# Mixer stage: late low parts of the GLU operand, an input quarter in the preparation's tile, a later residual write

## The chip, the cores and the metric

One core of a Trainium2 chip runs the whole program; the metric is the device time of one execution in microseconds. The core's engines run side by side: TensorE (PE, its weight loads as PEld), VectorE (DVE), ScalarE (ACT), GpSimd (POOL) and SyncE (SP), which issues most DMAs. Each engine takes its own instructions in a fixed order; semaphores tie the engines together.

## The reference

One step of a two-layer encoder over 1024 prompt and 64 sample positions, width 1024. Layer 0 has an attention mixer, layer 1 a diagonal state-space (SSM) mixer, then a GELU and a gated unit (GLU); each layer ends in a gated convolutional FFN. The part that matters here:

```python
    def block(carry, u_blk):
        ...
        _, _, sr, si = lax.associative_scan(_affine_combine, (ar, ai, xr, xi), axis=1)
        y = jnp.einsum('blgp,gip->blgi', sr, cr) - jnp.einsum('blgp,gip->blgi', si, ci)
        return (sr[:, -1], si[:, -1]), y
    ...
    y = ys.transpose(1, 0, 2, 3, 4).reshape(b, t, D_MODEL) + d_skip.astype(jnp.float32) * h.astype(jnp.float32)
    z = jax.nn.gelu(y).astype(h.dtype)
    ag = z @ w_glu + b_glu
    out = ag[..., :D_MODEL] * jax.nn.sigmoid(ag[..., D_MODEL:])
```

## The kernel before, in words

The stages follow one another: attention, first FFN (with the SSM tables prepared beside it, `ssm_prep`), SSM mixer with GLU (`ssm`), second FFN. Positions are cut into three blocks of 384, 384 and 320 columns. A float32 product is three matmuls on split operands: each operand x is kept as a high half (a rounded copy, made by ACT) and a low half (x minus the high half, made by DVE), and of the four partial products low·low is left out.

**Scan stage.** `batch` (L1236) works on one or two of 32 group pairs q; there are 18 batches: q=0, q=1, fourteen pairs from q=2 to q=29, q=30, q=31. `staged` runs several batches at once, each some `yield`s behind the one before. A batch's tables `pm` are loaded by SP (L1222); PE makes `p` from `pm` and the inputs U (L1258); ACT makes `sc` and `rd` (L1266, L1270); DVE makes `wk` by L1289, L1294, L1295, the scan at L1306, and L1309, L1310; PE multiplies out into the `p3` tiles (L1318, L1324); ACT copies them to `ys` (L1332). The inputs come as four quarters U(0) to U(3) of 16 groups (`ssm_load`, L1187); U(2) takes the slot `ypB`, which holds block 2 of the first FFN's output y until that block is written to DRAM as the residual ("spill", L1561, called in the batch q=2 round).

**From ys to the GLU operand.** After every four q (one `kt` of 0 to 7) ACT issues the write `yd` of `ys` (L1339), SP reads it back in another layout as `yf` (L1344), ACT forms z (GELU, L1359 and L1362) and its high half `zh` (three blocks, L1368), DVE its low half `zl` (three blocks, L1372). The DVE subtractions for kt 0 to 5 stand between scan instructions. The high and low halves (`whl`, L217) of the first two GLU weight tiles are made in the last scan rounds too.

**GLU.** For m = 0 the six first kt are multiplied for the three blocks with all three products, pb's weight first, then kt 6, then kt 7; the later m follow. The order on each engine comes from the order of the code and the `order` calls; the Tile framework adds waits where a buffer slot is taken again: a new tile in a slot waits until all readers of the last one are done.

**Preparation.** Its tiles `w`, `tl` and `tp` (L1058, L1100) are three separate tiles in the pool `prep2`, which nothing uses after the preparation.

## Time and profile before

| | us |
|---|---|
| median of 3 runs | 2240.37 |
| lowest, highest | 2238.83, 2241.77 |
| profiled execution: time | 2241.03 |
| profiled execution: span, first to last instruction | 2239.2 |

The profiled execution is one run, 0.66 us above the median; its span is what the trace covers and the rest (1.8 us) lies around it. Over the span PE is busy 98%, DVE 74%, ACT 47%, POOL 18%. The scan stage runs from about 1190 to 1294, the GLU follows. Averages over the span say little of this stage: it has to be read by windows and by the order of the instructions.

### The profile page before, as it was taken

The page shows a single profiled execution, that of the slowest core. Times are in us where ns is not written, and L with a number is a line of the kernel's source. Part 1 is how long each engine was busy: PE and PEld are TensorE (multiplying, and loading weights), DVE is VectorE, ACT ScalarE, POOL GpSimd, SP SyncE. Part 2 cuts the span into 40 slices and gives each one's busy share as a digit, 9 for nine tenths or more (in the row PEclk, how much of TensorE's full clock was granted, in tenths as well). Part 3 has the DMA queues.
Part 4 walks back from the last instruction along what each step waited for, and adds up shares of the span by engine and source line. Part 5 has one row for each costly group of instructions (what it writes and reads, how often), then busy time and mean ns, then how long its engine had stood idle before and what let it go on. Part 6 is the DMA issues. An engine that isn't in the chain of part 4 may idle for free.

```text
span 2239.2 us, 35982 instructions
## 1 busy us (share of the span) xinstructions
PE 2191.6 (98%) x13875; PEld 2117.1 (95%) x13875; DVE 1661.3 (74%) x2886; ACT 1042.3 (47%) x1890; POOL 412.8 (18%) x474
## 2 busy tenths in 40 slices
PE   9999999999999999999988899999999999999997
PEld 8987789999999999999986699999999999999997
DVE  8687647989878877767758855597976776676764
ACT  5255747422343342555545641263555455455543
POOL 5322004200032423000200034352010110110000
PEclk9999999999999999999999899999999999999999
DMA  5100015655355565887749888752266686579772
GB/s 197 37 22 29 20 62 158 241 188 202 122 150 173 176 208 187 274 279 236 233 163 339 263 280 294 249 167 75 87 224 229 218 297 226 196 272 314 218 253 97
DMA packets 208123, 428.47 MB, mean 191 GB/s; under 512 B 23312, under 2 KB 114224, under 8 KB 205008
## 3 DMA queue, kind: packets, MB, share of 16 engines
q1 hardware_dynamic: 175648, 326.56, 44.2%
q0 software_dynamic: 23984, 95.12, 11.9%
q10 hardware_dynamic: 8320, 4.49, 0.8%
q8 instruction: 109, 1.79, 0.3%
q14 instruction: 62, 0.51, 0.1%
HBM read 297.75 MB, written 128.37 MB: 190 GB/s over the span
## 4 chain that ended last, share of the span: by engine, by line
PE 32%; DMA 13%; DVE 9%; issue 4%; ACT 2%; POOL 2%; SPq 0%; DVEq 0%; ACTq 0%; POOLq 0%
PE mm L224 10%; PE mm L226 10%; PE mm L225 10%; DMA sj<-in_w_up 3%; DMA raw<-in_w_down 2%; DMA jw<-in_w_down 2%; DMA raw<-sd 1%; POOL sj L1391 1%; DMA yd<-ys 1%; DVE whl L217 1%; DMA su<-sj 1%; DMA gd<-t 1%; DVE gt L564 1%; DVE t L425 1%; DMA yf<-yd 1%
## 5 line engine op out<-in xcount | busy, mean ns | idle before, releaser
L224 PE MATMUL mm<-hl,whl 128*128 128x384 f32 (+1 forms) x1960 | 643.3, 329 | 4.1 <-DVE hl L307 3.1
L226 PE MATMUL mm<-hh,whl 128*128 128x384 f32 (+1 forms) x1960 | 641.2, 329 | 2.3 <-DVE whl L217 2.3
L225 PE MATMUL mm<-hh,whl 128*128 128x384 f32 (+1 forms) x1960 | 643.1, 328 | 0.0
L224 PEld LDWEIGHTS mm<-hl,whl 128*128 128x128 f32 x1960 | 368.4, 188 | 6.5 <-DVE hl L307 4.7
L226 PEld LDWEIGHTS mm<-hh,whl 128*128 128x128 f32 x1960 | 368.4, 188 | 3.0 <-DVE whl L217 2.9
L225 PEld LDWEIGHTS mm<-hh,whl 128*128 128x128 f32 x1960 | 368.6, 188 | 0.1
L217 DVE TENSOR_TENSOR whl<-raw,whl 128x1024 fp32r<-128x1024 f32 x202 | 254.9, 1263 | 146.7 <-ACT whl L217 146.2
L217 ACT ACTIVATE whl<-raw 128x1024 fp32r<-128x1024 f32 x202 | 213.0, 1058 | 248.1 <-PE mm L226 128.6
L224 PE MATMUL mm<-gt,whl 128*128 128x384 f32 (+1 forms) x968 | 316.8, 327 | 2.9 <-ACT whl L217 2.4
L226 PE MATMUL mm<-gt,whl 128*128 128x384 f32 (+1 forms) x968 | 315.8, 327 | 0.7 <-DVE whl L217 0.7
L225 PE MATMUL mm<-gt,whl 128*128 128x384 f32 (+1 forms) x968 | 315.9, 327 | 0.0
L224 PEld LDWEIGHTS mm<-gt,whl 128*128 128x128 f32 x968 | 181.7, 188 | 3.7 <-ACT whl L217 2.6
L226 PEld LDWEIGHTS mm<-gt,whl 128*128 128x128 f32 x968 | 181.7, 188 | 1.2 <-DVE whl L217 1.2
L225 PEld LDWEIGHTS mm<-gt,whl 128*128 128x128 f32 x968 | 181.8, 188 | 0.0
L195 DVE TENSOR_TENSOR whl<-raw,whl 128x1024 fp32r<-128x1024 f32 x84 | 96.4, 1154 | 72.7 <-ACT whl L194 71.3
L424 DVE SCALAR_TENSOR_TENSOR t<-u,ppt,t 128x1090 f32<-128x1090 f32 x88 | 126.9, 1443 | 5.8 <-ACT t L423 4.1
L194 ACT ACTIVATE whl<-raw 128x1024 fp32r<-128x1024 f32 x84 | 82.6, 987 | 101.8 <-DMA raw<-sd 40.1
L423 ACT ACTIVATE t<-u,ppt 128x1090 f32<-128x1090 f32 x88 | 114.2, 1298 | 26.2 <-DVE u L520 13.6
L425 DVE SCALAR_TENSOR_TENSOR t<-u,ppt,t 128x1090 f32<-128x1090 f32 x88 | 122.0, 1386 | 0.4
L415 DVE TENSOR_TENSOR u<-rb,mm 128x384 f32<-128x384 f32 (+1 forms) x164 | 80.8, 504 | 31.2 <-PE mm L226 26.4
L438 ACT ACTIVATE t<-t 128x1090 f32<-128x1090 f32 x44 | 49.1, 1115 | 113.1 <-DVE t L425 113.1
L564 DVE TENSOR_TENSOR gt<-gr,gt 128x768 fp32r<-128x768 f32 (+2 forms) x106 | 90.5, 881 | 11.1 <-ACT gt L563 10.2
(389 smaller groups left out, 4141.5 us busy)
## 6 DMA issues: line engine op xcount, KB each, us to landing
raw<-in_w_up SPq DMA_DIRECT2D x88, 512.0 KB, 4.4
raw<-in_w_down SPq DMA_DIRECT2D x74, 512.0 KB, 4.4
raw<-sd SPq DMA_DIRECT2D x40, 512.0 KB, 4.9
sj<-in_w_up POOLq DMA_DIRECT2D x68, 256.0 KB, 6.1
su<-sj POOLq DMA_DIRECT2D x34, 512.0 KB, 5.9
raw<-su SPq DMA_DIRECT2D x34, 512.0 KB, 4.6
pm<-prm SPq DMA_DIRECT2D x32, 522.0 KB, 8.2
gr<-td SPq DMA_DIRECT2D x40, 384.0 KB, 5.6
```

Source lines behind the costliest of these rows:

```text
L194: nc.scalar.activation(w[:, 0], raw, AF.Copy)
L195: nc.vector.tensor_sub(w[:, 1], raw, w[:, 0].bitcast(F32))
L217: x = nc.scalar.activation(w[:, 0], raw, AF.Copy), nc.vector.tensor_sub(w[:, 1], raw, w[:, 0].bitcast(F32))
L224: nc.tensor.matmul(out, w[:, 0, sl], xl, start=start, stop=False, skip_group_check=more)
L225: nc.tensor.matmul(out, w[:, 0, sl], xh, start=False, stop=False, skip_group_check=more)
L226: self.last_mm = nc.tensor.matmul(out, w[:, 1, sl], xh, start=False, stop=stop, skip_group_check=more)
L415: nc.vector.tensor_mul(u[:, t0 + 2:t0 + 2 + np_], rb[:, t0:t0 + np_], ps[:, :np_])
L423: nc.scalar.activation(t, u[:, 0:T + 2], AF.Identity, bias=cb(m), scale=cw(0, m))
L424: nc.vector.scalar_tensor_tensor(t, u[:, 1:T + 3], cw(1, m), t, op0=ALU.mult, op1=ALU.add)
L425: self.last_conv = nc.vector.scalar_tensor_tensor(t, u[:, 2:T + 4], cw(2, m), t, op0=ALU.mult, op1=ALU.add)
L438: nc.scalar.activation(ta, ta, AF.Gelu_apprx_tanh)
L564: nc.vector.tensor_sub(x[:, 1, u], raw, x[:, 0, u].bitcast(F32))
```

## The change

1. `w`, `tl`, `tp` become slices of one prep2 tile `p2`; U(2) is put in that slot instead of `ypB`, so its load no longer stands behind the spill.
2. The spill is issued in the batch q=24 round, behind the last `pm` load.
3. `LATE = (3, 4, 5)`: `zl` of these kt, and the low halves of the first two GLU weights, are made after the last scan instruction; z of kt 4 and 5 are put in the p2 slot.
4. GLU m = 0: first the high·high products of kt 0 to 5 for all three blocks, then the two other products.

```diff
 def split_unit(self, raw):
+        x = [nc.scalar.activation(w[:, 0], raw, AF.Copy)]
+        low = lambda: nc.vector.tensor_sub(w[:, 1], raw, w[:, 0].bitcast(F32))
+        if self.held is not None:
+            self.held.append(low)
+            return w
+        x.append(low())
...
-        w = self.prep2.tile([P, 4, 2, 16, 8], F32, name="w")
+        w = self.p2[:, 0].rearrange("p (g c j s) -> p g c j s", g=4, c=2, j=16)
...
-        tl, tp = (self.prep2.tile([P, 8, P], F32, name=x) for x in ("tl", "tp"))
+        tl, tp = (self.p2[:, x].rearrange("p (g f) -> p g f", g=8) for x in (1, 2))
...
         self.ssm_small()
+        self.p2 = self.prep2.tile([P, 3, 1024], F32, name="p2", tag="p2", bufs=1)
...
-            u = self.yp.tile([P, 16, NC_], F32, name="U", tag="ypB" if q == 2 else "ypA", bufs=1 if q == 2 else 2)
+            u = (self.prep2.tile([P, 16, NC_], F32, name="U", tag="p2", bufs=1) if q == 2
+                 else self.yp.tile([P, 16, NC_], F32, name="U", tag="ypA", bufs=2))
...
                 if qs[-1] == 31:
                     self.wsrc.pop(0)
+                    self.held = held
                     for j in range(AHEAD):
                         self.load_ahead(1 + j)
                         self.order(self.loaded, got[15])
+                    self.held = None
                 if qs[0] == 2:
-                    self.order(self.spill(), self.last_u)
                     us.append(self.ssm_load(2))
+                if qs[0] == 24:
+                    self.order(self.spill(), got[15])
...
-                    z = self.t4([P, T], "z")
+                    if kt == LATE[1]:
+                        late[:] = [self.prep2.tile([P, 2, T], F32, name="z", tag="p2", bufs=1)[:, x] for x in range(2)]
+                    z = late[kt - LATE[1]] if kt in LATE[1:] else self.t4([P, T], "z")
...
+                    if kt in LATE:
+                        zs[kt] = z
+                        return
...
             self.behind = out[0], ends[-1]
+            for low in reversed(held):
+                self.order(low(), ends[-1])
+            for b in range(3):
+                for k, z in zs.items():
+                    self.order(lower(b, k, z), ends[-1])
...
+                def products(ks, of=(0, 1, 2)):
...
+                            for j in of:
+                                e, x = ((0, zh), (1, zh), (0, zl))[j]
...
-                    products(range(k0))
+                    products(range(k0), (0,))
+                    yield
+                    products(range(k0), (1, 2))
                     yield
...
-            for x in order[:3]:
+            for x in order[:3] * 2:
                 next(x)
```

The list in which `late` is filled calls `prep2.tile` once for each of its two elements: z(4) and z(5) are two tiles that take the one slot in turn.

The order on three engines, before and in the changed program (the number at the end of a tile's name is that of the buffer; in the changed file the lines stand 1 to 33 lower).

SP, from the middle of the first table loads on. Before:

```order
L1222 DMA pm_11604<-prm_292 128x1044 x2
L1561 DMA x1_94<-y_10705 1024x1x320
L1222 DMA pm_11694<-prm_292 128x1044 x2
L1195 DMA U_11632<-hd_10756 128x8x137 x2
L1222 DMA pm_11751<-prm_292 128x1044 x2
L1344 DMA yf_11750<-yd_11541 128x1096
L1222 DMA pm_11807<-prm_292 128x1044 x2
L1222 DMA pm_11864<-prm_292 128x1044 x2
L1195 DMA U_11891<-hd_10756 128x8x137 x2
L1344 DMA yf_11863<-yd_11541 128x1096
```

In the changed program:

```order
L1231 DMA pm_11581<-prm_292 128x1044 x2
L1204 DMA U_11608<-hd_10733 128x8x137 x2
L1231 DMA pm_11670<-prm_292 128x1044 x2
L1231 DMA pm_11727<-prm_292 128x1044 x2
L1356 DMA yf_11726<-yd_11518 128x1096
L1231 DMA pm_11783<-prm_292 128x1044 x2
L1231 DMA pm_11840<-prm_292 128x1044 x2
L1356 DMA yf_11839<-yd_11518 128x1096
L1204 DMA U_11867<-hd_10733 128x8x137 x2
L1231 DMA pm_11911<-prm_292 128x1044 x2
```

U(2) (the first U row of each list) stands one place earlier, directly behind a pair of tables, and the write x1 that stood ahead of it is gone; the second `yf` (kt 1) stands ahead of U(3). Further on, the changed program has the write here:

```order
L1231 DMA pm_12155<-prm_292 128x1044 x2
L1231 DMA pm_12215<-prm_292 128x1044 x2
L1594 DMA x1_94<-y_10682 1024x1x320
L1356 DMA yf_12214<-yd_11518 128x1096
L210 DMA raw_12457<-in_w_glu 128x1024
L210 DMA raw_12461<-in_w_glu 128x1024
L1356 DMA yf_12331<-yd_11518 128x1096
L1356 DMA yf_12439<-yd_11518 128x1096
```

The write x1 stands behind the last tables and ahead of the `yf` of kt 4, and behind this come the first two GLU weights.

ACT, the end of the scan stage, with waits. Before (z of buffer 12495 is kt 5; the last two rows belong to q=30):

```order
L1339 DMA yd_11541<-ys_12412 128x8x137 [waits Activation_49]
L1359 ACTIVATE z_12495<-yf_12357 128x1024 [waits DMAHW1_49]
L1362 ACTIVATE z_12495<-yf_12357 128x64
L1368 ACTIVATE zh_11897<-z_12495 128x384 [waits Activation_49]
L1368 ACTIVATE zh_11900<-z_12495 128x384
L1368 ACTIVATE zh_11903<-z_12495 128x320 [waits Activation_49]
L1332 ACTIVATE ys_12525<-p3_12502 128x2x137 [waits DVE_49,PE_49]
L1332 ACTIVATE ys_12525<-p3_12503 128x2x137 [waits PE_49]
L1335 COPY fin_11574<-wk_12420 128x8 [waits DVE_49] x2
L1332 ACTIVATE ys_12525<-p3_12542 128x137 [waits PE_49]
L1332 ACTIVATE ys_12525<-p3_12543 128x137 [waits PE_49]
```

In the changed program (z of buffer 12357 is kt 5; the first two `ys` rows belong to q=30, the last two to q=31):

```order
L1344 ACTIVATE ys_12494<-p3_12508 128x137 [waits PE_49]
L1344 ACTIVATE ys_12494<-p3_12509 128x137 [waits PE_49]
L1347 COPY fin_11551<-wk_12443 128x4 [waits DVE_49] x2
L1373 ACTIVATE z_12357<-yf_12331 128x1024 [waits DMAHW1_49,DVE_49]
L1376 ACTIVATE z_12357<-yf_12331 128x64
L1382 ACTIVATE zh_11873<-z_12357 128x384 [waits Activation_49]
L1382 ACTIVATE zh_11876<-z_12357 128x384
L1382 ACTIVATE zh_11879<-z_12357 128x320 [waits Activation_49]
L1344 ACTIVATE ys_12494<-p3_12528 128x137 [waits PE_49]
L1344 ACTIVATE ys_12494<-p3_12529 128x137 [waits PE_49]
```

z(5) and its three `zh` have moved from ahead of the last `ys` of q=29 to between the `ys` of q=30 and of q=31, and z(5) now waits for DVE beside its DMA. That DVE value is the one set by the last subtraction of z(4), block 2.

DVE, from the scan of q=31 on. Before (from L1295 of q=31):

```order
L1295 TENSOR_TENSOR wk_12533<-wk_12533 128x2x137
L1306 SCALAR_TENSOR_TENSOR wk_12533<-rd_12432,wk_12533 128x276
L1372 TENSOR_TENSOR zl_11898<-z_12495,zh_11897 128x384
L1309 TENSOR_TENSOR wk_12533<-wk_12533,pm_12239 128x276
L1372 TENSOR_TENSOR zl_11901<-z_12495,zh_11900 128x384
L1372 TENSOR_TENSOR zl_11904<-z_12495,zh_11903 128x320
L1310 TENSOR_TENSOR wk_12533<-wk_12533,sc_12431 128x276
L1379 TENSOR_TENSOR fo_12600<-fin_11574 128x128
```

In the changed program (from the scan, here L1318):

```order
L1318 SCALAR_TENSOR_TENSOR wk_12502<-rd_12407,wk_12502 128x276
L1321 TENSOR_TENSOR wk_12502<-wk_12502,pm_12215 128x276
L1322 TENSOR_TENSOR wk_12502<-wk_12502,sc_12406 128x276
L220 TENSOR_TENSOR whl_12463<-raw_12461,whl_12463 128x1024
L220 TENSOR_TENSOR whl_12459<-raw_12457,whl_12459 128x1024
L1397 TENSOR_TENSOR zl_11874<-z_12243,zh_11873 128x384
L1397 TENSOR_TENSOR zl_11874<-z_12356,zh_11873 128x384
L1397 TENSOR_TENSOR zl_11877<-z_12243,zh_11876 128x384
L1397 TENSOR_TENSOR zl_11877<-z_12356,zh_11876 128x384
L1397 TENSOR_TENSOR zl_11880<-z_12243,zh_11879 128x320
L1397 TENSOR_TENSOR zl_11880<-z_12356,zh_11879 128x320
L1397 TENSOR_TENSOR zl_11874<-z_12357,zh_11873 128x384
```

After the last scan instruction (L1322) now come two weight halves, six subtractions of kt 3 and 4 (buffers 12243 and 12356), and then those of kt 5, which need zh(5) from ACT. The last of the six, block 2 of buffer 12356, is what z(5) waits for.

## Rows read from the trace of the kernel before

**Rows 1.** Cores: span (us) and mean granted TensorE clock.

```profile
core 0: 2239.2 us, clock 0.992
```

**Rows 2.** Windows (us, busy of PE, PEld, DVE, ACT, POOL with counts, PEclk, DMA share, GB/s).

```profile
1220.00:1240.00 20.00, 17.75 (x196) 14.12 (x194) 16.76 (x25) 9.89 (x24) 0.71 (x5) 1.00 1.07 338
1260.00:1280.00 20.00, 19.34 (x214) 15.43 (x212) 19.24 (x28) 16.37 (x39) 0.98 (x8) 1.00 0.85 255
...
1300.00:1320.00 20.00, 20.00 (x124) 20.00 (x123) 10.92 (x22) 9.17 (x12) 7.67 (x12) 1.00 0.86 307
```

**Rows 3.** Timeline of DVE, last rounds (start, duration, line, [idle <- releaser]).

```profile
1265.53 0.72 DVE L1289 TENSOR_TENSOR wk<-pm,p 128x548 f32<-128x548 f32 x1
...
1271.58 0.72 DVE L1289 TENSOR_TENSOR wk<-pm,p 128x548 f32<-128x548 f32 x1
...
1276.64 0.72 DVE L1289 TENSOR_TENSOR wk<-pm,p 128x548 f32<-128x548 f32 x1
...
1281.09 1.40 DVE L1372 TENSOR_TENSOR zl<-z,zh 128x384 fp32r<-128x384 f32 x3
1282.41 0.72 DVE L1309 TENSOR_TENSOR wk<-wk,pm 128x552 f32<-128x552 f32 x1
...
1283.82 0.43 DVE L1289 TENSOR_TENSOR wk<-pm,p 128x274 f32<-128x274 f32 x1
...
1284.52 1.22 DVE L217 TENSOR_TENSOR whl<-raw,whl 128x1024 fp32r<-128x1024 f32 x1
1285.66 0.44 DVE L1295 TENSOR_TENSOR wk<-wk 128x274 f32<-128x274 f32 x1
```

**Rows 4.** Timeline of DVE, rounds of batches q=12 and q=16.

```profile
1224.24 0.72 DVE L1289 TENSOR_TENSOR wk<-pm,p 128x548 f32<-128x548 f32 x1
...
1228.95 1.03 DVE L1372 TENSOR_TENSOR zl<-z,zh 128x384 fp32r<-128x384 f32 x2 [2.52 <-ACT zh L1368]
...
1232.90 0.72 DVE L1289 TENSOR_TENSOR wk<-pm,p 128x548 f32<-128x548 f32 x1
...
1238.22 0.72 DVE L1289 TENSOR_TENSOR wk<-pm,p 128x548 f32<-128x548 f32 x1
...
1244.88 1.03 DVE L1372 TENSOR_TENSOR zl<-z,zh 128x384 fp32r<-128x384 f32 x2 [4.47 <-ACT zh L1368]
...
1248.84 0.72 DVE L1289 TENSOR_TENSOR wk<-pm,p 128x548 f32<-128x548 f32 x1
```

**Rows 5.** Timeline of ACT in the second of these rounds.

```profile
1242.19 2.04 ACT L1359 ACTIVATE z<-yf 128x1024 f32<-128x1024 f32 x1 [8.01 <-DMA yf<-yd]
...
1245.52 0.66 ACT L1332 ACTIVATE ys<-p 128x274 f32<-128x274 f32 x2
```

**Rows 6.** Waits of the SP queue, 1195 to 1300 (total us, times, longest).

```profile
SPq L1344 <- DMA yd<-ys: 26.9, 6, 8.1
...
SPq L1195 <- DMA x<-y: 6.1, 1, 6.1
```

**Rows 7.** DMA issues, 1195 to 1295 (count, KB each, median us to landing).

```profile
yf<-yd SPq DMA_DIRECT2D x7, 548.0 KB, 5.4
...
x<-y SPq DMA_DIRECT2D x1, 1280.0 KB, 13.4
```

**Rows 8.** Timeline, all engines, end of the scan stage.

```profile
1291.51 0.44 DVE L1310 TENSOR_TENSOR wk<-wk,sc 128x276 f32<-128x276 f32 x1
...
1293.92 0.46 ACT L1332 ACTIVATE ys<-p 128x137 f32<-128x137 f32 x2 [1.57 <-PE p L1324]
...
1294.44 0.44 PE L224 MATMUL pb<-zl,whl 128*128 128x384 f32 x1 [0.55 <-ACT ys L1332]
```

**Rows 9.** Windows as in rows 2, around the last fall of the TensorE clock.

```profile
1283.00:1290.00 7.00, 6.71 (x41) 5.81 (x42) 6.65 (x14) 2.96 (x9) 0.41 (x3) 0.51 0.76 233
1290.00:1293.00 3.00, 3.00 (x30) 2.26 (x30) 1.94 (x5) 0.64 (x4) 0.00 (x0) 1.00 0.11 41
```

**Rows 10.** Waits of PE, 1165 to 1320 (total us, times, longest).

```profile
PE p L1324 <- DVE wk L1309: 3.5, 4, 2.1
```

More of the change, by code (lines that the diff above doesn't have):

```diff
@@ L37 @@
 SUMMED = (0, 0, 1, 1, 1, 1, 0)
+LATE = (3, 4, 5)
 NC_ = 137
@@ L212 @@
     behind = ()
+    held = None
     def split_unit(self, raw):
@@ L216, in split_unit @@
         w = self.big([P, 2, D], "whl")
-        x = nc.scalar.activation(w[:, 0], raw, AF.Copy), nc.vector.tensor_sub(w[:, 1], raw, w[:, 0].bitcast(F32))
+        x = [nc.scalar.activation(w[:, 0], raw, AF.Copy)]
[4 more added lines that the diff above has]
+        x.append(low())
         for u, v in zip(x, self.behind):
@@ L1368, in batch, with lower @@
                         nc.scalar.activation(zh[b][:, kt], z[:, t0:t0 + n_], AF.Copy)
+                    if kt in LATE:
+                        zs[kt] = z
+                        return
                     if kt < 7:
                         yield
-                    for b, (t0, n_) in enumerate(BLK):
-                        x = nc.vector.tensor_sub(zl[b][:, kt], z[:, t0:t0 + n_], zh[b][:, kt].bitcast(F32))
+                    for b in range(3):
+                        x = lower(b, kt, z)
                         if kt < 7:
                             self.order(x, adds[-1])
+            late, zs, held = [], {}, []
+            def lower(b, k, z):
+                t0, n = BLK[b]
+                return nc.vector.tensor_sub(zl[b][:, k], z[:, t0:t0 + n], zh[b][:, k].bitcast(F32))
             scans, ends = [], []
@@ L1377, in ssm @@
             self.behind = out[0], ends[-1]
+            for low in reversed(held):
+                self.order(low(), ends[-1])
+            for b in range(3):
+                for k, z in zs.items():
+                    self.order(lower(b, k, z), ends[-1])
             fo = sp.tile([P, P], F32, name="fo")
@@ L1419, in tile_ @@
                 pa, pb = self.mm_ps("pa"), self.mm_ps("pb")
-                def products(ks):
+                def products(ks, of=(0, 1, 2)):
                     for ps, w in ((pb, ws[m][1]), (pa, ws[m][0])):
                         for k in ks:
-                            self.mm3(ps[:, :n], w, slice(k * P, (k + 1) * P), zh[b][:, k], zl[b][:, k], k == 0, k == KD - 1)
+                            for j in of:
+                                e, x = ((0, zh), (1, zh), (0, zl))[j]
+                                nc.tensor.matmul(ps[:, :n], w[:, e, k * P:(k + 1) * P], x[b][:, k], start=k == 0 and j == 0,
+                                                 stop=k == KD - 1 and j == 2)
                 k0 = 0
```

## The prediction

> **What bounds the kernel now.** I first read the span and clock of the core: 2239.2 us at 0.992 of the full clock, so nothing disturbs the whole run [rows 1]. Then windows of 20 us, to find which engine is full where. From 1300 on PE is busy 20.00 of 20 us; in the scan stage it isn't, while DVE has 19.24 of 20 us in 1260 to 1280 [rows 2]. So DVE sets the pace of the scan, and what comes behind it is set by PE: there a start of the GLU that is later by 1 us is an end that is later by 1 us, as no idle time is left to take it up. I therefore look for two moments: D, the end of DVE's last scan instruction (1291.51 + 0.44 = 1291.95), and G, the first GLU matmul (1294.44). G is D + 2.49, through the last `ys` copy of ACT, which the matmul waits for [rows 8].
>
> In the timeline of DVE a plain round of two q takes 1276.64 - 1271.58 = 5.06 us; a round with one `zl` trio (1265.53 to 1271.58) 6.05 [rows 3]. Two rounds are much longer: 1224.24 to 1232.90 is 8.66 and 1238.22 to 1248.84 is 10.62; in them DVE stands idle for 2.52 and 4.47 us for `zh` of ACT [rows 4]. ACT had itself been idle, 8.01 us in the second case, for the DMA `yf` [rows 5]. SP shows what is behind that: it waited 26.9 us for `yd` writes before it could issue their `yf`, and 6.1 us with U(2) behind the spill [rows 6]. The spill is 1280 KB and took 13.4 us to land [rows 7], and the DMA engines were full then: share 1.07 at 338 GB/s in 1220 to 1240 against 0.85 in 1260 to 1280 [rows 2].
>
> **The change part by part.**
>
> *Low parts out of the scan.* A `zl` trio holds DVE for 1282.41 - 1281.09 = 1.32 us, a weight's low half for 1285.66 - 1284.52 = 1.14 [rows 3]. Not all of it is gained, since some filled handover gaps: the trio of kt 3 cost 6.05 - 5.06 = 0.99; the round of q=28, with a trio and a low half (2.46), took 1283.82 - 1276.64 = 7.18, or 2.12 too much [rows 3]. The q=30 and q=31 rounds hold as much again, 2.12 to 2.46; I take 2.2. Together D comes 0.99 + 2.12 + 2.2 = 5.3 us earlier.
>
> *The two stalls.* They make their rounds 8.66 - 6.05 = 2.61 and 10.62 - 6.05 = 4.57 us longer, 7.2 in all, which bounds the gain; the other end is nothing. At 338 GB/s the spill's 1280 KB are 3.9 us of the engines' time, and these now fall behind the first `yf`, which needs to come 2.5 us earlier. The second must come 2.6 + 4.5 = 7.1 earlier; it has the spill's 3.9 and the two U(3) loads, which it now passes and which each have the size of a `yf` (548 KB [rows 7], so 3.3 us for both). That is 7.2: just enough. I take 6.2 of the 7.2.
>
> *The spill late.* It now stands behind the last tables and ahead of the `yf` of kt 4. There the engines have room (0.85), but the two fewer stalls press the same loads into less time. At least it costs nothing, at most its 3.9 us of bytes, if ACT sits on z(4) with the weights' high halves and the next `sc` and `rd` queued behind, for which DVE waits. I take 1. Its own reader comes much later, in the GLU's end.
>
> So D moves by -5.3 - 6.2 + 1 = -10.5.
>
> *What now stands between D and G.* z(4) and z(5) are two tiles in one slot, so z(5) waits until DVE has subtracted the last block of z(4), and this has been put behind the last scan instruction, two low halves and five other subtractions. On ACT the `ys` of q=31 is queued behind z(5) and its `zh`, and PE's first GLU matmul needs that `ys`. The chain from D: two low halves 2 x 1.14, two trios 2 x 1.32, so 4.92; z(5) with its tail and three `zh` 1245.52 - 1242.19 = 3.33 [rows 5]; the `ys` pair to the first matmul 1294.44 - 1293.92 = 0.52 [rows 8]. G = D + 8.77 in place of D + 2.49: +6.3 us. All of it is on the path, and PE has nothing else queued ahead of the GLU.
>
> *The clock.* PE is then idle from its last p3 matmul (about D + 1.9, just ahead of the `ys` at 1293.92 [rows 8]) to D + 8.8, nearly 7 us. Before, waits of up to 2.1 us for L1309 [rows 10] were enough: in 1283 to 1290 the granted clock is 0.51, the 1.2 GHz level, and from 1290 on 1.00 again [rows 9]. Such a 7 us stretch, all of it over dense matmuls, would lose 3.4 us; nothing if it lay in the idle time. As the idle ends where the densest matmuls begin, I take 2.6, nearer the upper end. The Trainium skill ("TensorE: Matmul & The Clock Gate", section "HAM oscillation — how this bites in real kernels") puts the price of a throttled stretch at its length times one minus the clock ratio, and speaks against a change that opens such a gap. By it alone, with the whole stretch counted, the sum would be 0.8 us worse than mine.
>
> *High products first.* The GLU's matmuls are as many as before. The 36 high products at 20/124 = 0.161 us each [rows 2] are 5.8 us of work, in which DVE makes the `zl` of kt 5 (1.32, from about G - 0.5 on): no wait, no gain on this path. Were that cover gone, the trio would cost at most 1.3. The second pair of weights is loaded later too, but is needed only after the 144 matmuls of m = 0, some 23 us behind G.
>
> Sum: -10.5 + 6.3 + 2.6 = **-1.6 us** against the profiled 2241.03, so 2239.4; that execution lies 0.66 above the median, so **2238.8 us**. With 0 to 4 us of stalls left in all and 1 to 3.4 us for the clock, this case spans 2235 to 2242.
>
> **The rivals.**
>
> *The wait of z(5) costs nothing* (z(4)'s subtractions are done in time, or the matmuls start by themselves). Then G stays D + 2.5 and the clock holds: 2241.03 - 10.5 - 0.66 = 2229.9. For it speaks that the high products were put first, so that PE can begin without the low parts. Against it stands the order of DVE: the awaited subtraction is behind the last scan instruction. Chance 0.14.
>
> *The DMA engines stay the bound*, and the change is slower. The bytes of the stage are the same; the spill only changes places with U(2) and U(3). Then the 7.2 us of stalls stay, or come back in later rounds (share 1.07 in the first half, and 0.85 for the second before its time is cut [rows 2]), and the spill in front of the `yf` of kt 4 adds its 3.9: -5.3 + 3.9 + 6.3 + 2.6 = +7.5, so 2247.9. It decides the sign as soon as over 3.6 us of stalls are left (-5.3 - 7.2 + 3.6 + 8.9 = 0), and slower by more than I can tell from no change at about 8. Against it: SP's order shows the first two `yf` with fewer bytes ahead. The Trainium skill ("DMA: Bandwidth & Descriptors", section "Issuing engines are not separate DMA queues") says that DMAs of all issuing engines run on the same 16 engines and interleave, which is this rival's ground. The share of 1.07 agrees that they fill up. Chance 0.18.
>
> *A longer fall of the clock.* The idle of 7 us is longer than any here, and the GLU may begin with the half level for a full stretch and part of another: 5 to 6 us in place of 2.6, so about 2242. Chance 0.10.
>
> **How the numbers follow.** The forecast keeps 0.58. A measurement of this kernel tells about 0.2% (4.5 us) from no change: faster is below 2235.9, slower above 2244.9. Faster: the first rival, 0.14, and a tenth from the low edge of the forecast (no stall left, small clock price): 0.24. Slower: nearly all of the second rival and 0.03 of the third and the forecast's high edge: 0.20. The rest, 0.56, is the same. The range 2231 to 2246 leaves out about 0.09 below and 0.1 above.
>
> **What would show it.** In the new profile: plain rounds of 5.06 us without trios behind q=24; no idle of DVE over 1 us for `zh` in the first half; D near 1281; then PE idle for 6 to 7 us, waiting for `ys` of ACT, with z(5) directly ahead of it released by DVE's `zl`; a granted clock of about 0.5 in the first microseconds of the GLU, and after it the same lengths as before. A GLU start within 4 us of D would make the forecast wrong on the fast side; idle of DVE for `zh` or `sc` of over 6 us in all, on the slow side.

## The result and the profile after

The changed kernel takes **2247.02 us** (median of 9 runs, 2244.23 to 2251.02), the kernel before 2236.8 us beside it: ratio 1.0043, 95% interval [1.0033, 1.0053], so it is slower by 7.4 to 11.9 us. The forecast was 2238.8, no change, and its range ended at 2246. The profiled execution took 2250.79 us, 9.8 more than that of before; each lies about 4 us above the median of the nine runs of its kernel (3.8 and 4.2). First its core (span, mean granted clock):

```profile
core 0: 2249.0 us, clock 0.990
```

I set the same moments in both traces: t1, the start of the first round of two q (1198.39 before, 1202.31 now); D, the end of DVE's last scan instruction (1291.95 and 1295.34); G, the first GLU matmul (1294.44 and 1304.13); and the end.

| stretch, us | before | after | difference |
|---|---|---|---|
| start to t1 | 1198.39 | 1202.31 | +3.9 |
| t1 to D (forecast -10.5) | 93.56 | 93.03 | -0.5 |
| D to G (forecast +6.3) | 2.49 | 8.79 | +6.3 |
| G to the end (forecast +2.6) | 944.8 | 944.9 | +0.1 |

The first line is work that the change leaves in the same order. Over the 19 profiles of this study t1 lies between 1194.9 and 1203.2, for kernels with and without the new tile, so it may be the spread of single executions; that it is nothing else is not shown (see "What is left" below). What the change does to this stage stands in the two lines in the middle.

The windows of the changed kernel (us, busy time and count of PE, PEld, DVE, ACT, POOL, PE's granted clock, DMA share, GB/s):

```profile
1220.00:1240.00 20.00, 18.72 (x212) 15.19 (x213) 19.11 (x27) 12.90 (x34) 0.76 (x6) 1.00 0.90 246
1240.00:1260.00 20.00, 16.79 (x174) 13.37 (x172) 15.57 (x23) 12.38 (x32) 0.83 (x6) 0.91 1.05 320
1260.00:1280.00 20.00, 20.00 (x232) 16.45 (x230) 18.96 (x27) 11.67 (x33) 0.89 (x7) 1.00 1.00 286
1280.00:1300.00 20.00, 12.18 (x106) 9.62 (x102) 13.04 (x23) 10.04 (x29) 0.58 (x4) 0.74 0.53 175
```

Where before the DMA engines had 0.85 in 1260 to 1280 [rows 2], they now have 1.00, and 1.05 ahead of it; the slice of 1220 to 1240 that held the stalls fell from 1.07 to 0.90. DVE, full in 1220 to 1240, has 15.57 of 20 us in the next window and 13.04 in the last, in which the scan ends. Its timeline shows why (start, duration, line, [idle <- releaser]):

```profile
1231.40 1.02 DVE L1397 TENSOR_TENSOR zl<-z,zh 128x384 fp32r<-128x384 f32 x2
...
1242.76 1.02 DVE L1397 TENSOR_TENSOR zl<-z,zh 128x384 fp32r<-128x384 f32 x2
...
1258.24 1.03 DVE L1397 TENSOR_TENSOR zl<-z,zh 128x384 fp32r<-128x384 f32 x2 [3.56 <-ACT zh L1382]
...
1272.56 0.72 DVE L1301 TENSOR_TENSOR wk<-pm,p 128x548 f32<-128x548 f32 x1
...
1277.61 0.71 DVE L1301 TENSOR_TENSOR wk<-pm,p 128x548 f32<-128x548 f32 x1
...
1289.08 0.44 DVE L1301 TENSOR_TENSOR wk<-pm,p 128x274 f32<-128x274 f32 x1 [6.34 <-ACT fin L1347]
...
1294.89 0.45 DVE L1322 TENSOR_TENSOR wk<-wk,sc 128x276 f32<-128x276 f32 x1
```

The two stalls of before [rows 4] are gone: the first two `zl` wait for nothing. A round without `zl` takes 1277.61 - 1272.56 = 5.05, as forecast. But the third `zl` waits 3.56, and the round of q=30 waits 6.34 for ACT. ACT's timeline at that place:

```profile
1282.98 2.02 ACT L1373 ACTIVATE z<-yf 128x1024 f32<-128x1024 f32 x1 [8.71 <-DMA yf<-yd]
...
1285.11 1.28 ACT L1382 ACTIVATE zh<-z 128x384 fp32r<-128x384 f32 x3
1286.30 1.99 ACT L219 ACTIVATE whl<-raw 128x1024 fp32r<-128x1024 f32 x2
1288.19 0.66 ACT L1344 ACTIVATE ys<-p 128x274 f32<-128x274 f32 x2
1288.75 0.30 ACT L1347 COPY fin<-wk 128x8 f32<-128x8 f32 x2
```

ACT sits on z(4), 8.71 us, until its `yf` has landed; two weight halves, `ys` and `fin` stand in order behind it, and DVE waits for that `fin`. SP's longest wait is what delays the `yf` (waits of SP, 1195 to 1300: total, times, longest; then the landing times of the `yd` writes from issue):

```profile
SPq L1356 <- DMA yd<-ys: 49.6, 7, 12.0
```

```profile
DMA to landing us min/median/max: 4.4/9.8/13.1
```

SP waited 26.9 us for `yd` before [rows 6], now 49.6. The longest, 13.1, is the write of kt 4: issued at 1262.32, just behind one pair of tables and 3.6 us ahead of the next. Its `yf`, issued at 1275.51, 8.6 us behind the spill, then took 7.4 us.

The end of the scan, all engines:

```profile
1297.53 2.76 DVE L1397 TENSOR_TENSOR zl<-z,zh 128x384 fp32r<-128x384 f32 x6
...
1300.32 2.03 ACT L1373 ACTIVATE z<-yf 128x1024 f32<-128x1024 f32 x1 [2.28 <-DVE zl L1397]
...
1303.64 0.44 ACT L1344 ACTIVATE ys<-p 128x137 f32<-128x137 f32 x2
...
1304.13 1.28 PE L1454 MATMUL pb<-zh,whl 128*128 128x384 f32 x3 [4.56 <-ACT ys L1344]
```

This is the chain that was forecast: z(5) starts 4.98 us after D, released by DVE's `zl`, its last `ys` 3.32 later, the matmul 0.49 after that.

### The profile page after: what moved, and what is told of

Same layout as the page of the kernel before. It is cut to its first block, busy times and chain, and to the rows that moved or that the text cites. A ratio compares the mean times of both kernels' runs of the same rounds, so it can differ in the third digit from the quotient of the medians.

```text
span 2249.0 us, 35985 instructions
## 1 busy us (share of the span) xinstructions
PE 2192.6 (97%) x13875; PEld 2119.3 (94%) x13875; DVE 1661.6 (74%) x2886; ACT 1041.7 (46%) x1890; POOL 414.8 (18%) x474
## 4 chain that ended last, share of the span: by engine, by line
PE 40%; DMA 10%; DVE 7%; ACT 3%; issue 2%; SPq 1%; POOL 0%; ACTq 0%; DVEq 0%; POOLq 0%
PE mm L231 10%; PE mm L233 10%; PE mm L232 10%; PE pb L1454 4%; PE pa L1454 4%; DMA raw<-in_w_down 4%; DMA yd<-ys 1%; DVE whl L220 1%; DMA pm<-prm 1%; ACT whl L219 1%; DMA gd<-t 1%; DVE y L336 1%; DMA raw<-sd 1%; DMA gr<-gd 1%; DVE whl L196 1%
## 5 line engine op out<-in xcount | busy, mean ns | idle before, releaser
L1454 PE MATMUL pb<-zh,whl 128*128 128x384 f32 (+1 forms) x384 | 95.5, 331 | 4.6 <-ACT ys L1344 4.6
```

What stands on the lines that cost most here:

```text
L1454: nc.tensor.matmul(ps[:, :n], w[:, e, k * P:(k + 1) * P], x[b][:, k], start=k == 0 and j == 0, stop=k == KD - 1 and j == 2)
```

## The experiments

Each was timed beside the kernel before, whose median was 2237.8 to 2239.3 us there, so the ratios are what to compare; run 12 is a single execution. A profile is one execution and can lie several us off the median. "Stretch" is t1 to D in the profile, "handover" D to G, "GLU" G to the end.

**1. Two halves of one tile.** So that z(5) doesn't wait for z(4)'s readers.

```diff
-late[:] = [self.prep2.tile([P, 2, T], F32, name="z", tag="p2", bufs=1)[:, x] for x in range(2)]
+pair = self.prep2.tile([P, 2, T], F32, name="z", tag="p2", bufs=1)
+late[:] = [pair[:, x] for x in range(2)]
```

> The changed kernel with z of kt 4 and 5 as the two halves of one tile, so that z(5) no longer waits for the subtractions of z(4). Everything else is the change. First theory (two causes: the wait of z(5), 6.3 us between the last scan instruction D and the first GLU matmul G, with 1.7 us of half clock behind it; and the spill ahead of the yf of kt 4, 6.3 us of DVE idle before q=30): G - D falls from 8.8 to 2.5 us, the idle before q=30 stays at 5 to 7, the clock is full at the start of the GLU; the time is 7 to 8 us below the changed kernel, so 2 to 3 us above before. Rival (the wait is covered: something else, the GLU's weights or low parts, would hold the start as long): G - D stays above 5 us and the time within 3 us of the changed kernel, 7 to 10 above before.

2240.77 us, 1.0013 [1.0000, 1.0026]. Handover 4.85 in place of 8.79 (I had expected 2.5), stretch 89.2, and DVE still waits ahead of q=30:

```profile
1286.19 0.44 DVE L1301 TENSOR_TENSOR wk<-pm,p 128x274 f32<-128x274 f32 x1 [5.09 <-ACT fin L1347]
```

So the wait of z(5) is worth 6 us of the 9.6, and what remains is still not faster than before: most of the scan's own gain is missing too.

**2. The spill back in the third round**, ahead of U(2).

```diff
 if qs[0] == 2:
+    self.order(self.spill(), self.last_u)
     us.append(self.ssm_load(2))
-if qs[0] == 24:
-    self.order(self.spill(), got[15])
```

> The changed kernel with the write of the residual's block 2 back in the q=2 round ahead of U(2); U(2) stays in the preparation's place and the z(5) wait stays. First theory (the late spill itself makes the 6.3 us idle before q=30): that idle is under 1 us; the first two waits for zh come back in part, 0 to 5 us together, and the time is 2 to 6 us below the changed kernel, 4 to 8 above before. Rival (the DMA engines are the bound of the whole stage; where the spill stands does not matter): the idle of DVE over the scan stage stays at 10 to 12 us in all, only in earlier rounds, and the time is within 1.5 us of the changed kernel, 9 to 11 above before.

2245.41 us, 1.0032 [1.0015, 1.0049]; handover 8.79, stretch 91.5. The stop before q=30 falls to 2.55, but one of 5.13 stands earlier. The late spill is a small part of the loss at most.

**3. The preparation's places alone**: `w`, `tl` and `tp` as slices of one `p2` tile in the kernel before.

```diff
+self.p2 = self.prep2.tile([P, 3, 1024], F32, name="p2", tag="p2", bufs=1)
-w = self.prep2.tile([P, 4, 2, 16, 8], F32, name="w")
+w = self.p2[:, 0].rearrange("p (g c j s) -> p g c j s", g=4, c=2, j=16)
-tl, tp = (self.prep2.tile([P, 8, P], F32, name=x) for x in ("tl", "tp"))
+tl, tp = (self.p2[:, x].rearrange("p (g f) -> p g f", g=8) for x in (1, 2))
```

> The kernel before with one edit of the change: the preparation's three tiles as slices of one. Scan and GLU as before. The profile of the changed kernel reached the scan stage 4 us later than that of before. First theory (that lateness is the spread of single executions): within 1.5 us of before, and the first scan round within 1.5 us of 1198.4 in its profile. Rival (the shared tile slows the first FFN beside which the preparation runs): 3 to 4 us above before, with the scan's first rounds 3 to 5 us late.

2239.68 us, 1.0009 [0.9995, 1.0022], t1 at 1199.8: no cost that can be told, though the interval reaches up to 4.9 us.

**4. One tile, and the spill behind the scan's last `yf` but one.**

```diff
-if qs[0] == 24:
-    self.order(self.spill(), got[15])
 ...
+self.order(self.spill(), yfs[6])
 self.behind = out[0], ends[-1]
```

> The changed kernel with one z tile for kt 4 and 5 (as the run before with that edit) and the write of the residual behind the yf of kt 6, so after the scan's own loads. First theory (both causes taken away): idle before q=30 under 1 us, G - D 2.5 to 3 us, D some 6 us earlier than with the late spill; the time is 13 to 15 us below the changed kernel, 3 to 5 below before. Rival (the DMA engines are the bound): DVE's idle of 6 us turns up at other rounds, and the time is only 7 to 8 us below the changed kernel, 2 to 3 above before.

2242.6 us, 1.0018 [1.0003, 1.0033]. DVE's wait ahead of q=30 is still 5.41 with no spill near (it goes out at 1289.57); the `yd` of kt 4 took 13.5 us. So that write is slow beside the tables alone. The gain of 3 to 5 us that I had expected without both causes did not come.

**5. The write of the scan's output in whole rows**, one tile as in run 1.

```diff
-out.append(nc.scalar.dma_start(yd[kt * P:kt * P + P].rearrange("(g i) t c -> (i t) g c", i=16), ys[0]))
+out.append(nc.scalar.dma_start(yd[kt * P:kt * P + P], ys[0]))
```

> The run with one z tile, and the write of yd made in the order of the partitions (whole rows of 4384 bytes instead of pieces of 548): the same bytes and the same waits, but the values that z and the GLU get are permuted. First theory (the DMA engines are full, and the write in small pieces loses against the tables' large ones, so that yf of kt 4 comes too late for ACT): yd lands in 5 to 7 us in place of 10, DVE's idle after the second round is under 2 us in place of 7.4, from the first pair's round to D 82 to 84 us in place of 89; the time is 5 to 8 us below the run with one z tile, 2 to 6 below before. Rival (the bytes alone count, or ACT's order): yd stays at 9 us or more, the idle before q=30 at 3 us or more, and the time within 2 us of the run with one z tile.

This write leaves out the reordering of the output, so it prices the transfer and is no version to keep. 2234.57 us, 0.9980 [0.9966, 0.9995]. Stretch 83.4, waits of DVE in it 2.1 in all. The landing times of its `yd` writes, and DVE ahead of q=30:

```profile
DMA to landing us min/median/max: 2.7/7.1/9.3
```

```profile
1274.80 0.44 DVE L1301 TENSOR_TENSOR wk<-pm,p 128x274 f32<-128x274 f32 x1 [1.33 <-ACT fin L1347]
```

The same bytes, instructions and order on ACT, with the late spill where the change has it: between these two executions the pieces of the write alone make 5.8 us of the stretch. The forecast's stretch was 93.56 - 10.5 = 83.1. But the profile of run 5 is that of its fastest execution, 2228.35 us, 6.2 below its median, so 83.4 is a low value.

**6. The moves alone**: U(2) in the preparation's place and the spill late, but all low parts in the scan.

```diff
-LATE = (3, 4, 5)
+LATE = (9, 9, 9)
-                    self.held = held
```

> U(2) in the preparation's place and the spill behind the last tables, as in the change, but all low parts and the GLU as before. First theory (the stage is bound by its transfers, so waits move rather than vanish): the two waits for zh of 2.5 and 4.5 us shrink, but 2 to 6 us of idle of DVE turn up at kt 2 or at q=30; the time is -3 to +3 us from before. Rival (the moves do take the waits away): DVE's idle after the second round under 1.5 us, from the first pair's round to D 87 to 88 us in place of 93.6, 5 to 7 us below before.

2238.6 us, 1.0006 [0.9994, 1.0019]. Stretch 96.8, with a wait of 6.39 of DVE: the `yd` of kt 4 took 13.4 us and the spill 14.2. So the moves alone bring the late stop, without any low part moved; the time is that of before.

**7. The low parts alone**: U(2) and the spill as before, one tile.

```diff
-u = (self.prep2.tile([P, 16, NC_], F32, name="U", tag="p2", bufs=1) if q == 2
-     else self.yp.tile([P, 16, NC_], F32, name="U", tag="ypA", bufs=2))
+u = self.yp.tile([P, 16, NC_], F32, name="U", tag="ypB" if q == 2 else "ypA", bufs=1 if q == 2 else 2)
 ...
```

> The low parts late and the GLU's high products first, with one z tile; U(2) and the spill as before. First theory (transfers bind: a DVE that has less to do waits more): the waits at the first two zh stay (5 to 8 us) and one of 2 to 4 us comes before q=30; from the first pair's round to D 89 to 91 us, G - D 2.5 to 4.5; the time is -3 to +2 us from before. Rival (the low parts are worth their 5.3 us): no new wait before q=30, the time 4 to 6 us below before.

2240.32 us, 1.0006 [0.9993, 1.0020], though the stretch is 87.1 and G is at 1288.28, 6 us earlier than before. DVE's two stalls for `zh` stay, at 3.2 and 2.4 us, and no late one comes. The gain is gone at the GLU's end, 952.7 us of GLU in place of 944.8. DVE and PE there:

```profile
1435.93 0.43 DVE L1422 TENSOR_TENSOR sj<-sj 128x256 f32<-128x256 f32 x1 [4.77 <-DMA sj<-in_w_up]
...
1442.01 0.61 DVE L1469 SCALAR_TENSOR_TENSOR y<-pa,ppt,sg 128x384 f32<-128x384 f32 x1
```

```profile
1445.14 1.01 PE L274 MATMUL pr<-ones,sqa 128*128 128x1 f32 x4 [5.41 <-DVE sqa L268]
```

The sums for w_up are made beside the GLU, 68 loads `sj` in a chain of POOL, DMA and DVE. DVE takes them in order with the GLU's last `y`, so PE waits 5.41 us for the chain, which makes 5.1 of the 7.9 us; the rest I did not trace. The chain lasts 141 us from the first issue (1299.01) to the last landing (1440.27); in the kernel before also 141 (1300.47 to 1441.27), and PE waited 0.3 us there. Scan and sums were nearly level: a GLU that begins earlier gains nothing unless the sums end earlier.

**8. One tile, spill at the end, each `yf` issued ahead of another pair of tables.**

```diff
-if t + 6 in got:
-    self.order(x, got[t + 6])
+if t + 5 in got:
+    self.order(x, got[t + 5])
 ...
```

> The run with one z tile and the spill at the end, and each yf issued one pair of tables earlier, so that SP holds that pair back until yd has landed. First theory (the tables in flight are what slows yd, and they have rounds to spare): yd lands in 5 to 8 us, the idle before q=30 is under 2 us, from the first pair's round to D 83 to 86 us; the time is 4 to 8 us below the run without this edit, 1 to 5 below before. Rival (the tables have no time to spare, the engines' total is the bound): PE and ACT wait for pm by as much, and the time is within 2 us of the run without the edit.

2245.77 us, 1.0029 [1.0017, 1.0041]; stretch 92.1. Now z waits for no `yf`. But ACT, which had no such wait in run 4, waits three times, 15.3 us in all, for a `yd` to land before it can write a `ys`, and DVE's waits for ACT's `fin` rise from 5.4 to 9.1. PE's waits for tables are 7.9 us, against 7.2 in run 4, so that the tables have no time to spare is not shown. The writes of kt 1 to 4 still take 8.8 to 10.3 us.

**9, 10 and 11. The last `yd` ahead of the second weights on ACT**, to start the sums' chain earlier: in the kernels of run 7, of run 1, and of run 1 with the spill of run 2.

```diff
-self.behind = out[0], ends[-1]
+self.behind = out[-1], ends[-1]
```

> The run with the low parts alone, and on ACT the write yd of kt 7 ahead of the high halves of the second pair of GLU weights (it stood behind them, and they wait for loads that wait for the late low halves). First theory (in the run without this edit the GLU began 6 us earlier than before, but yd of kt 7 went out 6.6 us after D in place of 2.5; the loads sj of GpSimd begin only when it has landed, pace the stage's end, and gave back 8 us there): yd of kt 7 goes out within 1 us of G, sj begins 6 us after G, no wait of PE over 1 us at the end of the GLU, G to the end 943 to 946 us; the time is 5 to 7 us below the run without the edit, 3 to 6 below before. Rival (the loads sj are held by the transfers, whatever starts them): G to the end stays 950 to 953 us, and the time within 1.5 us of the run without the edit.

> The change with one z tile and the same edit on ACT (yd of kt 7 ahead of the second weights). First theory: G - D and the idle before q=30 as in the run with one z tile (4 to 5 us and 4 to 7 us), G to the end 943 to 945.5 us without a wait at the end of the GLU; the time is 0 to 2 us below that run, 1 to 3 above before: the stall before q=30 is what is left. Rival (with this the whole change is a gain): 3 us or more below before.

> The same with the spill back ahead of U(2), which stays in the preparation's place: only the residual's write is not moved. First theory (not the spill's place but the phase of the tables' loads to yd of kt 4 makes the stall before q=30): that idle 2 to 5 us, the first two zh waits 4 to 7 together, D no earlier than with the spill late by more than 2 us; the time is within 2.5 us of the run with the spill late and the same edits. Rival (the late spill makes the stall): no idle over 1 us before q=30, and 3 to 6 us below that run.

2242.24 (1.0009 [0.9998, 1.0020]), 2243.66 (1.0018 [1.0005, 1.0030]) and 2241.59 us (1.0008 [0.9996, 1.0021]). In run 9 `yd` goes out 2.7 us earlier and the first `sj` 0.6, and PE's stop at the GLU's end stays 5.29 us. Run 10 has its wait ahead of q=30 again, 6.55 us, and run 11 a stretch of 87.4 and a stop of 3.3. The trace of run 9 says why so little moved (waits of POOL, 1290 to 1445):

```profile
POOL sj L1418 <- DMA yd<-ys: 3.2, 1, 3.2
```

The first `sj` waits until the last `yd` has landed, and that write took 7.8 us here in place of 5.7. In all 19 profiles the first `sj` goes out 0.5 to 0.8 us behind that landing, and in nine of them the profile names it as the releaser. So the write does hold the start of the chain, but by its landing, which an earlier issue moved by 0.6 us only.

**12. The changed kernel again**, as it is.

> The changed kernel once more, unchanged, for a second profile. First theory (its waits are of the order, and the 4 us by which the first profile reached the scan late are the spread of one execution): G - D 8.7 to 8.9 us, an idle of DVE of 4 to 7 us before q=30, the first pair's round anywhere between 1195 and 1203. Rival (the lateness before the scan is of this program): the first pair's round again at 1202 to 1204.

Handover 8.79, the wait ahead of q=30 8.75, t1 at 1203.0, 2252.21 us. The handover repeats, and so does the wait, 2.4 us longer. This t1 fits both theory and rival, so it decides nothing.

**13 and 14. The state's write behind the second load of the sums**, in the kernels of runs 7 and 11.

```diff
-            nc.gpsimd.dma_start(a["o_st"], fo)
 ...
                 beside()
+                if len(loaded) == 2 and fo is not None:
+                    nc.gpsimd.dma_start(a["o_st"], fo)
+                    fo = None
```

> The seventh run's kernel (low parts late alone), with one edit: the write of the final state is emitted behind the second of the loads for the w_up sums (sj) instead of ahead of the first, so that on GpSimd's queue no sj load stands behind fo, which is added behind the late low parts. In the seventh run the scan's gain was lost at the GLU's end, where TensorE stood 5.4 us for sums whose loads had come last. Theory, the sums' chain is late because its start stands behind the state's write: the first sj load is issued some 4 us earlier, the stop at the GLU's end falls to 0 to 2 us, the stretch from the GLU's first matmul to the end is 946 to 949 us (952.7 there), and the time 2234 to 2237 us. Rival, the chain's end is set by how fast its 68 loads are moved, or by the buffers that free late: the first load moves, the last one doesn't, the stop stays at 4 us or more, 2239 to 2242 us.

> The eleventh run's kernel (the change with the two late z tiles as halves of one tile, the spill back in the third round's place, and the last write of the scan's output ahead of the second unit's weight highs on ScalarE), with the same edit: the state's write behind the second sj load. There the scan took 87.4 us from the first pair round and TensorE stopped 3.3 us at the GLU's end. Theory, the start of the sums' chain stands behind the state's write: the stop goes to under 1 us, 947 to 949 us behind the GLU's first matmul (951.6 there), 2236 to 2239 us. Rival, the transfers set the chain's end: the stop stays at 3 us or more, 2240 to 2243 us.

2239.55 (1.0008 [0.9995, 1.0021]) and 2244.66 us (1.0031 [1.0017, 1.0045]): no gain. In run 13 the first `sj` didn't move (1299.82, 0.6 us behind the landing of `yd` again), so an earlier start was not tried there; PE's stop fell to 2.3 all the same, as the chain took 138 us. In run 14 it came 3.1 us earlier than in run 11; the last landing came 2.2 earlier, as G did, and the stop was 3.8. So an earlier start alone didn't shorten the stop. The chain took 143 us there and 142 in run 11, but over the 19 profiles it takes 137 to 147, so whether the transfers set its length is not shown.

**15. Rows written, pieces read**: the full output, the `yf` in eight reads of 548-byte pieces.

```diff
-x = nc.sync.dma_start(yf, yd[kt * P:kt * P + P])
+x = [nc.sync.dma_start(yf[16 * g:16 * g + 16], yd[kt][:, g].rearrange("(i t) c -> i t c", t=8)) for g in range(8)][-1]
```

> The change with the two late z tiles as halves of one tile, and the scan's output written to DRAM in whole partition rows of 4384 bytes (as in the fifth run), but read back in its proper order: eight reads of 16 partitions each, in pieces of 548 bytes, in place of one read in whole rows. The output is the full one. Theory, a transfer in small pieces is the one that falls behind beside the large table loads, on whichever side the pieces are: the write takes about 7 us as in the fifth run, the eight reads together 10 to 13 us in place of 5, so the same wait of z for yf comes back around the fifth and sixth, 88 to 92 us from the first pair round to the scan's end and 2239 to 2244 us. Rival, only a write in small pieces is slow: write 7 us and reads 5 to 7 us, 83 to 86 us for that stretch, 2233 to 2237 us.

2257.71 us, 1.0096 [1.0077, 1.0114]. Written in rows `yd` takes 5.6 us (median). But the eight reads of kt 4 go out from 1268.08 to 1277.21, with two tables and the spill between them on SP, and the last lands at 1283.20, 15.1 us after the first; DVE waits 11.3 us ahead of q=30. The time that the rival gave did not come, but how much of it is the pieces and how much the eight issues, this run doesn't tell apart.

**16 and 17. Rows in the kernel before, and rows in the change as it is**: run 5's edit alone.

> The kernel before, with the fifth run's edit alone: the scan's output goes to DRAM in whole partition rows of 4384 bytes and not in pieces of 548, so that what is read back is permuted and the output is not the reference's; all instructions and bytes stay. It asks what the late low parts are worth once the write is out of the way. Theory, the write in pieces was the limit of the scan before too, and VectorE's two stops of 2.5 and 4.5 us were its face: they go, the stretch from the first pair round to the scan's end falls from 93.6 to 86 to 88 us, and the time to 2230 to 2234 us, no worse than the fifth run (2234.6), so that the edit and not the change's moves gives the gain. Rival, before the change VectorE's own stream was the limit and the rows' write shows only in a shorter stream: the stretch stays at 91 us or more and the time at 2236 to 2240 us.

> The changed kernel with the same edit alone (write in whole rows, output permuted), the two late z tiles still two tiles of one slot. Theory: the scan is as short as in the fifth run (83 to 86 us from the first pair round to its end, no stop ahead of the round of q = 30), and what is left of the change's loss is the wait of z(5) for z(4)'s last subtraction: from the scan's end to the GLU's first matmul 8.5 to 9 us, 6 to 7 us more than in the fifth run, 2239 to 2243 us. Rival, the wait of z(5) lies beside the late write alone and vanishes with it: 2 to 4 us behind the scan's end, 2233 to 2237 us.

Run 16: 2233.93 us, 0.9981 [0.9970, 0.9992], stretch 87.6, both stalls gone, one wait left (waits of DVE, 1205 to 1292):

```profile
DVE zl L1372 <- ACT zh L1368: 1.1, 1, 1.1
```

It is as fast as run 5: the write in rows brings the whole gain, and the low parts, with which the profile shows a stretch 4 us shorter still (83.4), bring nothing to the end that can be measured; the two intervals leave room for some 4 us either way. By the ratios the rows are worth 4.3 us in the kernel before (run 16), 7.4 on run 1 (run 5) and 8.3 on the change (run 17). Run 17: 2239.61 us, 1.0006 [0.9994, 1.0018]. Its handover is 8.79 again, so the wait of z(5) is a loss of its own, 5 us against run 5. Its stretch, 89.6, missed my 83 to 86. DVE and ACT of run 17:

```profile
1280.89 0.44 DVE L1301 TENSOR_TENSOR wk<-pm,p 128x274 f32<-128x274 f32 x1 [5.72 <-ACT fin L1347]
```

```profile
1274.76 2.06 ACT L1373 ACTIVATE z<-yf 128x1024 f32<-128x1024 f32 x1 [5.84 <-DMA yf<-yd]
```

Here the `yd` of kt 4 took 7.1 us, but its `yf` was issued 1.8 us behind the late spill and took 10.5. So the spill in front of that `yf` can hold it too, which runs 4 and 6 had left open: in the seven profiles with the late spill there the `yf` of kt 4 takes 7.4 to 10.5 us (median 7.8), in eleven others 3.5 to 7.5 (median 4.5; run 15 left out).

No version that writes the full output was faster than the kernel before.

## Why the prediction was wrong

Against the forecast of -1.6 us the profile shows +9.8: 10.0 of the difference lies between t1 and D, 3.9 ahead of t1, and the clock took 2.5 less than I gave it.

*Low parts out of the scan, -5.3: right.* Plain rounds take 5.05, and in run 7, without the moves, the stretch falls by 6.5, of which 1.4 are shorter stalls. The rounds of q=30 and 31 take 1295.34 - 1289.08 = 6.26 us, from 1291.95 - 1283.82 = 8.13 before: -1.9 (I took 2.2).

*The stalls and the late spill, -6.2 + 1: wrong, and this is the step that failed.* I wrote that "the engines have room (0.85), but the two fewer stalls press the same loads into less time", and took 1 us for it. The two stalls did vanish (7.0 us of idle). But in place of -5.2, DVE's waits of over 1 us from t1 to D rose from 2.52 + 4.47 = 7.0 to 1.24 + 3.56 + 6.34 = 11.1, so +4.1: that uses up nearly all of the low parts' gain, and -0.5 is left. The rival "the DMA engines stay the bound" came true, with stalls in later rounds at a share of 1.00; its 7.2 + 3.9 = 11.1 us of stalls are what was measured. That its 2247.9 is 0.9 from the median is luck in part: its clock term was 2.5 too high, the 3.9 ahead of t1 were in no sum, and the kernel before came out 3.6 lower beside the change than the 2240.37 I had started from. Its mechanism was only half mine. In the runs it is the write `yd` in small pieces among the tables: in rows all three kernels are faster (runs 5, 16, 17), and the one profile of run 5 has the forecast's stretch. The spill in front of the `yf` of kt 4 adds to it (run 17), but isn't needed (run 4). "DVE sets the pace of the scan" was wrong too: run 16 takes 6 us out of the stretch with every instruction of DVE as it was. I had priced the engines by bytes, and let `yd` keep its pace, when the sign stood in the trace of before. ACT's wait of 8.01 us [rows 5] stands behind the `yd` of kt 1, as the chain of before shows:

```profile
1219.25 14.41 DMA yd<-ys
1233.68 8.43 DMA yf<-yd
1242.19 2.04 ACT z L1359
```

The waits of SP for `yd`, 26.9 us [rows 6], are no sign by themselves; run 5 has 38.9, and DVE hardly waits there.

*What stands between D and G, +6.3: right* to 0.02 us: 8.79 against 8.77, and in run 1 most of it goes away.

*The clock, +2.6: too high.* Windows of after around the GLU's first matmuls:

```profile
1284.00:1294.00 10.00, 5.38 (x28) 4.28 (x28) 4.44 (x10) 7.49 (x21) 0.58 (x4) 0.50 0.34 117
1295.00:1304.00 9.00, 4.57 (x48) 3.53 (x44) 6.29 (x12) 5.20 (x16) 0.00 (x0) 1.00 0.55 181
1304.00:1308.00 4.00, 3.87 (x13) 3.87 (x14) 2.98 (x5) 4.00 (x6) 0.55 (x1) 0.57 0.73 169
1308.00:1312.00 4.00, 4.00 (x27) 4.00 (x26) 1.57 (x4) 2.64 (x6) 1.89 (x3) 1.00 0.74 215
```

PE's idle was 4.56 us and not nearly 7: PE had itself stood 7.39 us for ACT's `ys` until 1288.62, the clock was at half, 1.2 GHz, in 1284 to 1294, and at D it still had the last two matmul groups to do. Behind G the clock is 0.57 in 1304 to 1308 and 1.00 in the next window; 0.43 of 4 us is 1.7 us of work. The whole stretch from G to the end lost only 0.1, so 1.6 came back behind it; where, I did not trace. The rival of a longer fall did not happen.

*"A start of the GLU that is later by 1 us is an end that is later by 1 us": right in that direction, wrong in the other.* Run 7 starts the GLU 6 us earlier and ends no earlier, since its sums start only 1.5 us earlier; in the profile of run 5 they start 9 us earlier, and PE doesn't stop for them. What releases them is the landing of the last `yd`: 10.1 us behind G in run 7, 7.0 in run 5, where that write is in rows and takes 2.9 us, and 5.3 before. I saw no idle time behind G and did not ask how near the next producer was to becoming late.

*What is left.* +6.3, -0.5 and +0.1 make 5.9 of the 9.8 in the profile, and the interval is 7.4 to 11.9, so some 4 us have no shown cause. Run 12's wait ahead of q=30 is 2.4 us longer, so the stops vary from one execution to another. Both profiles of the change have a late t1 (1202.3 and 1203.0), where run 17, in the same order up to there, has 1197.5. In 860 to 1065, far ahead of the scan, PE is idle for 0.5 us before, 3.0 and 2.4 in the two profiles of the change, and 1.0 in run 17. Whether that is chance or a cost of the preparation's one tile, for which run 3 leaves room, is open.

## What to carry to other kernels

When instructions are taken from the engine that looks full, look first at which transfer its waits end on, and price that transfer beside the load it will meet when the same bytes fall in less time. A write of small pieces can be the limit while its bytes are few. Two tiles in one slot make the second wait for the first's last reader, so before readers are put late, count what is queued behind the second on its engine; and before a stage is shortened, see how late the next producer beside it already is.

## What the runs showed of the hardware

I had not expected what the size of the pieces costs. The same 548 KB with no other transfer under way take 2.7 us in rows of 4384 bytes and 4.4 in pieces of 548 (the `yd` of kt 6 in run 5 and in the change). Among the tables the longest `yd` of a profile is 7.0 to 9.3 us in rows (runs 5, 15, 16, 17) and 10.3 to 14.4 in pieces (the other fifteen). The windows 1205 to 1285 (as above) of the change and of run 5:

```profile
1205.00:1285.00 80.00, 69.85 (x750) 56.62 (x750) 69.77 (x96) 44.84 (x118) 3.23 (x25) 0.95 0.99 302
```

```profile
1205.00:1285.00 80.00, 75.31 (x826) 61.34 (x825) 74.70 (x108) 54.74 (x147) 3.49 (x27) 1.00 0.87 302
```

At the same 302 GB/s the DMA engines are busy 0.99 of the time with pieces (0.96 in run 3) and 0.87 with rows. The Trainium skill ("DMA: Bandwidth & Descriptors", section "Specifications") names 512 bytes as the least transfer for full rate; these pieces lie above it and still cost 1.6 times as long alone, so the measurement decides. The same page ("Queues, rings and completion order") says that a DMA engine takes its queues in turn, packet by packet. That would fit a write of many small pieces falling behind wide rows of tables, but no run here shows the turns themselves.
